# One hybrid diffusion-transformer step: the two softmax maps of a differential head subtracted ahead of the product with the values

## The chip, the cores and the metric

The kernel runs on one core of a Trainium2 chip. The metric is device time in microseconds (us) of one execution. The program of before takes 1923.86 us (median of 3 runs, 1923.54 to 1925.37).

## What is computed

One inference step of a two-layer backbone on 128 context tokens and 512 latent tokens, model width 1024. Layer 0 mixes eight heads of latent attention (MLA) with four heads of differential attention; layer 1 mixes grouped-query and neighbourhood attention. Each layer ends with a gated feed-forward part of width 2816. The change lies in the differential heads. Their reference, cut to what matters (head of two 64-wide query and key halves c, values 128 wide, per-head norm behind):

```python
def diff_attend(q, k, v, lam):
    scale = q.shape[-1] ** -0.5
    def block(qb):
        s = jnp.einsum('bqhcd,bthcd->bhcqt', qb, k).astype(jnp.float32) * scale
        p = jax.nn.softmax(s, axis=-1)
        a = (p[:, :, 0] - lam * p[:, :, 1]).astype(v.dtype)
        return jnp.einsum('bhqt,bthd->bqhd', a, v)
    return map_query_blocks(block, q)
```

The latents (512 queries) read 640 keys, five tiles of 128. The context tokens read only context tokens, in a separate small part that the change leaves as it is.

## The kernel before

Attention of layer 0 is `attention("att0", ...)` over eight jobs, each a pair of maps: D0 to D3 are the four differential heads (a pair is the two maps of a head), M0 to M3 are pairs of MLA heads. Iteration i of its loop works on three pairs side by side: the maxima of pair i+1 (`max_steps`: PE writes a product into PSUM as `pm`, DVE reduces it, L503), the scores of pair i (`score_steps`: PE writes transposed scores `st`, key tile by 512 queries, L546; ACT writes their exponentials into `p`, two key tiles to one 128x1024 tile, or `ps` for the fifth tile, L558; POOL adds the five tiles of a map into `ac`, L562 and L565), and the values of pair i-1 (`value_steps`, PE, L615). The order on each engine follows the order of the calls, with a tile framework's own scheduling on top: each iteration has six stages, and in each come two maxima, a sixth of the scores, one step of the values (the string 'xxsv' of `CFG`), then a step of the list `lag` and a piece of the adaLN products (`ada`, L300 and L307), which are fillers.

For a differential head before, both maps have a value product of their own: `po` of map 0 and of map 1, five products each of a 128x128 by 128x512 tile in f32, each of which the trace shows as two matmul records. `fin` copies both with ACT (L624, and L629 into the tile `dt`). Softmax sums come one or two iterations after the values: `norm_steps`, once for D0 and D1 and once for D2 and D3, makes the sums `su` on PE with the weights `ones` (L643), inverts them on DVE (L650), splits the reciprocals into a high and a low part (ACT L160, DVE L161), spreads them to all partitions with PE (`bcast`, `bc`, L658 and L659, 128x512), multiplies `o` and `dt` by them (L666, L667) and adds minus lambda times the second to the first (L668). The per-head norm of the output (`pr.after`: `sub` with the parts `ps_sub` L248, `pc_sub` L265, `pb_sub` L273 on PE, then L1065 and L1066 on DVE) follows on the same list.

PSUM has two kinds of tiles here: `pmm` (two banks: `pm`, `st`, `qs`) and `psm` (one bank: `po`, `su`, `bc`, `qt`, `qo`, the parts of `sub`, `ada`); all come from one pool of eight banks, given out in the order of the calls. The weight tiles `wt` (`wr`, `wm`, `wh`, `wl`, twelve buffers) hold streamed weights elsewhere in the program and `p` and `ac` in the attention.

```python
            for m, mp in enumerate(pr.maps):
                pj, s, e = mp.p[kt]
                out = pr.po[m] if pr.diff else pr.po[0][64 * m : 64 * m + 64]
                PE.matmul(out[:, s:e], mp.v(kt), pj, start=(i == 0), stop=(i == 4))
```

Of the kernel before, what the change touches and what calls it, by code (L numbers as in the profile page):

```python
# [35 lines left out]
WMB = 4  # L36
# [20 lines left out]
def tile_step(ctx: ExitStack, tc: tile.TileContext, a: dict):  # L57
# [23 lines left out]
    def psm(name, kind="sm"):  # L81
        """One bank of PSUM; kinds may share a ring, each phase of the step in its own way."""
        tag, bufs = banks[kind]
        return pq.tile([128, 512], F32, tag=tag, name=name, bufs=bufs)
# [7 lines left out]
    def place(shape):  # L92
        """A view of the tile that stays."""
# [10 lines left out]
    def ring(tag, cols, bufs, dt=F32):  # L104
        """The next of a ring of views of the tile that stays."""
# [7 lines left out]
    def wt(tag, name, dt=F32):  # L113
        if tag in ("k4", "rope32"):
            return dr(name, dt)[:, 0:1024]
        return rp.tile([128, 1284], dt, tag=tag, name=name, bufs={"wr": 2, "wm": WMB}.get(tag, 3))[:, 0:1024]
# [15 lines left out]
    # ---------------------------------------------------------------- constants  # L132
# [11 lines left out]
    # ---------------------------------------------------------------- projections  # L144
# [24 lines left out]
    def halves(pt, m=128, e=0, cut=HALF):  # L169
        """The two banks of a pair hold the halves so that all 640 columns, and e more before them, are contiguous."""  # L170
        return pt[:m, 512 - cut - e : 512], pt[:m, 512 : 512 + NT - cut]
# [21 lines left out]
    def proj_pair(pts, wss, xs, e, cut):  # L193
        """Two chunks whose first halves come before their second halves."""
# [10 lines left out]
    def chunks(items, u, first_pair):  # L205
        """items: (weights, name, evacuate) per chunk of 128 columns over the model width."""
# [18 lines left out]
    # ---------------------------------------------------------------- norms  # L225
# [3 lines left out]
    class Sums:  # L229
        """Sums of squares over features: chunk i of total accumulates in psum quadrant i % 4."""  # L230
# [48 lines left out]
    # ---------------------------------------------------------------- adaLN  # L279
# [6 lines left out]
    def adaln_steps(l, b, wide=False):  # L286
        """256 columns of w_mod: a fourth of the rows of each half sits in each column tile of the array."""
# [25 lines left out]
    def adaln(l, v):  # L313
        """One of the six vectors: shift, scale, gate of the mixer, then of the ffn."""
# [5 lines left out]
    def mod_scale(l, i, c0=0, c1=8):  # L320
        """A = norm_w * (1 + scale) of sub-layer i (0: attention, 1: ffn)."""
# [3 lines left out]
    def mod_gate(l, i):  # L325
        """G = gate * norm_w of the norm after sub-layer i."""
# [3 lines left out]
    def regions(cut):  # L330
        """Both parts of the tokens, split by kind."""
# [5 lines left out]
    def square_h(h, hf, cut, name):  # L337
        """Sums of squares of a part of the residual stream."""
# [9 lines left out]
    def residual(h, y, ysums, hf, cut):  # L348
        """h += y / rms of a part of the tokens, where y has its gate already; y is lost."""
# [32 lines left out]
    class Raw:  # L382
        """The scaled residual stream before its norm, after the shifts of both kinds of tokens as two
        columns: a product with it times the reciprocal root mean square, plus the product of the
        shift, is the product with the modulated norm."""
# [30 lines left out]
    # ---------------------------------------------------------------- start: residual stream, first adaLN group  # L416
# [35 lines left out]
    # ---------------------------------------------------------------- small vectors  # L452
# [17 lines left out]
    def lam_column():  # L470
        """-lambda = exp(l2 . l3) - exp(l0 . l1) - lambda_init on every partition."""
# [19 lines left out]
    # ---------------------------------------------------------------- attention of a pair of maps  # L491
    def max_steps(pr):
        """Row maxima of the scores of a pair of maps, negated, into their query tiles."""
# [11 lines left out]
        def near(m, qts):  # L505
            """Two query tiles with as many keys: context keys, then those of the neighbourhood with their bias."""
# [1071 lines left out]
def _masks():  # L1578
# [4 lines left out]
    out = []  # L1583
# [125 lines left out]
```

## Time and profile before

| what | value |
|---|---|
| median of 3 runs | 1923.86 us |
| range of the runs | 1923.54 to 1925.37 us |
| span of the profiled execution | 2037.7 us (28995 instructions) |
| PE busy | 1983.5 us, 97% |
| PE weight loads busy | 1666.1 us, 82% |
| DVE busy | 1016.9 us, 50% |
| ACT busy | 799.6 us, 39% |
| POOL busy | 206.1 us, 10% |
| mean granted clock of PE | 0.836 |

The profiled execution has no time of its own beside its span; its span is 1.059 times the median of the runs. A duration of the trace becomes a duration of a run by the inverse of that, 0.944. Busy shares are means over the whole program; attention of layer 0 lies between about 200 and 440 us of the span, its differential heads between about 245 and 355 us, and the rows behind the prediction come mostly from there. In the views, a PE row such as "x4 2.18" groups four matmul records that follow each other and 2.18 us from the first start to the last end; the cost of the group is the distance to the start of the next row. A bracket behind a row gives how long the engine was idle before it and what ended that.

### The profile page before, as it was taken

To read this page: it belongs to the slowest core of one execution; us is meant where nothing else is said; L and a number is where in the kernel's file an instruction comes from. 1 tells how busy PE (TensorE), PEld (TensorE's weight loads), DVE (VectorE), ACT (ScalarE), POOL (GpSimd) and SP (SyncE) were. 2 spreads that over 40 slices of the span, in tenths; PEclk is the share of its full clock that TensorE was granted. 3 is DMA by queue.
4 is the path that set the end of the run, shared out by engine and by line. 5 is a ranking of instruction groups with operands and counts; after the bars stand their busy time and mean duration, and the time that the engine had idled before them with its cause. 6 is when DMAs were issued, how large, how long until landed. Compare 5 with 4: busy or idle time off the path is not lost. (4 is left out here: it accounts for less than half of the span.)

```text
span 2037.7 us, 28995 instructions
## 1 busy us (share of the span) xinstructions
PE 1983.5 (97%) x11715; PEld 1666.1 (82%) x11715; DVE 1016.9 (50%) x1776; ACT 799.6 (39%) x1325; POOL 206.1 (10%) x205
## 2 busy tenths in 40 slices
PE   7999799999999999999999999999999999999997
PEld 4888555568799999999978985456879999999995
DVE  3353554463664563653645543435266456365454
ACT  3432233244543442442465422324364344144243
POOL 0010243330100000000010003630010000000000
PEclk7888788888888888888888887888888888888887
DMA  7445654242212324332323354573322221311221
GB/s 267 160 155 185 169 138 117 63 165 94 83 64 88 112 73 151 109 105 92 110 72 130 112 172 149 151 205 106 116 83 82 75 93 41 105 58 58 80 71 52
DMA packets 84103, 229.89 MB, mean 113 GB/s; under 512 B 12225, under 2 KB 24897, under 8 KB 83969
## 3 DMA queue, kind: packets, MB, share of 16 engines
q1 hardware_dynamic: 74656, 209.73, 32.6%
q10 hardware_dynamic: 6720, 7.82, 1.4%
q0 software_dynamic: 2592, 10.49, 1.3%
q8 instruction: 92, 1.51, 0.3%
q14 instruction: 43, 0.34, 0.1%
HBM read 198.82 MB, written 28.06 MB: 111 GB/s over the span
## 5 line engine op out<-in xcount | busy, mean ns | idle before, releaser
L186 PE MATMUL pu<-uop,wh_u 128*128 128x322 f32 (+1 forms) x2688 | 536.0, 323 | 0.0
L186 PEld LDWEIGHTS pu<-uop,wh_u 128*128 128x128 f32 x2688 | 445.9, 193 | 6.6 <-issue 5.2
L186 PE MATMUL pu<-uop,wl_u 128*128 128x322 f32 x1344 | 322.7, 323 | 0.0
L1333 DVE SCALAR_TENSOR_TENSOR za<-za,cst 128x127 f32<-128x127 f32 (+1 forms) x528 | 193.1, 435 | 96.7 <-ACT za L1325 96.6
L186 PEld LDWEIGHTS pu<-uop,wl_u 128*128 128x128 f32 x1344 | 233.5, 191 | 0.0
L186 PE MATMUL dn<-g,wh_d 128*128 128x320 f32 x1088 | 215.8, 323 | 0.0
L186 PEld LDWEIGHTS dn<-g,wh_d 128*128 128x128 f32 x1088 | 179.8, 192 | 1.0 <-issue 1.0
L269 POOL TENSOR_TENSOR cst<-cst 128x3 f32<-128x3 f32 (+2 forms) x23 | 23.7, 1032 | 1299.2 <-DVE cst L267 1295.9
L414 ACT ACTIVATE za<-za,cst 128x128 f32<-128x128 f32 (+1 forms) x176 | 89.3, 555 | 111.0 <-DVE za L412 102.0
L160 ACT ACTIVATE wh_u<-wr_u 128x1024 fp32r<-128x1024 f32 x88 | 92.1, 1052 | 102.8 <-PE dn L186 55.3
L186 PE MATMUL dn<-g,wl_d 128*128 128x320 f32 x544 | 130.4, 322 | 0.0
L161 DVE TENSOR_TENSOR wl_u<-wr_u,wh_u 128x1024 fp32r<-128x1024 f32 x84 | 102.2, 1217 | 22.7 <-ACT wh_u L160 22.6
L186 PEld LDWEIGHTS dn<-g,wl_d 128*128 128x128 f32 x544 | 94.7, 191 | 0.0
L411 DVE COPY cst<-pu 128x2 f32<-128x2 f32 x88 | 13.9, 158 | 160.2 <-PE pu L186 154.6
L1325 ACT ACTIVATE za<-za,cst 128x640 f32<-128x640 f32 x88 | 81.2, 923 | 2.9
L160 ACT ACTIVATE g<-za 128x640 fp32r<-128x640 f32 x44 | 32.5, 739 | 123.4 <-DVE za L1364 123.4
L1380 DVE TENSOR_TENSOR yf<-yf,dn 128x640 f32<-128x640 f32 x32 | 26.3, 821 | 105.4 <-PE dn L186 105.4
L160 ACT ACTIVATE wh_d<-wr_d 128x768 fp32r<-128x768 f32 (+1 forms) x48 | 38.0, 803 | 90.6 <-PE dn L186 71.7
L412 DVE TENSOR_TENSOR za<-pu,rnuop 128x640 f32<-128x640 f32 x88 | 71.7, 815 | 0.0
L300 PE MATMUL ada<-wm,cst 128*32 128x256 f32 x768 | 68.7, 436 | 2.0 <-ACT psD L558 1.2
L1359 ACT ACTIVATE za<-za 128x640 f32<-128x640 f32 x44 | 32.5, 739 | 94.1 <-DVE za L1333 94.1
L161 DVE TENSOR_TENSOR wl_op<-wr_op,wh_op 128x1024 fp32r<-128x1024 f32 x26 | 31.7, 1223 | 69.1 <-ACT wh_op L160 63.7
(579 smaller groups left out, 3595.4 us busy)
## 6 DMA issues: line engine op xcount, KB each, us to landing
wm<-in_wmod SPq DMA_DIRECT2D x96, 512.0 KB
wr_u<-in_w_up SPq DMA_DIRECT2D x88, 512.0 KB
wr_op<-in_w_o SPq DMA_DIRECT2D x26, 512.0 KB
wr_d<-in_w_dn SPq DMA_DIRECT2D x32, 384.0 KB
wr_dl<-in_w_dn SPq DMA_DIRECT2D x24, 320.0 KB
wr_d<-in_w_dn SPq DMA_DIRECT2D x16, 320.0 KB
h<-in_xT SPq DMA_DIRECT2D x4, 640.0 KB
hb<-in_xT SPq DMA_DIRECT2D x4, 640.0 KB
```

Of the source, the lines that this page charges most:

```text
L160: ACT.activation(hi, src, AF.Copy)
L161: low.tensor_tensor(lo, src, hi, op=ALU.subtract)
L186: PE.matmul(o[hf], w, xhalf(x, hf, e), start=start, stop=stop)
L269: POOL.tensor_tensor(r[:, :nt], ms[:, :nt], mhalf.to_broadcast([128, nt]), op=ALU.pow)
L300: PE.matmul(st["pt"][32 * j : 32 * j + 32, 0:256], silu_c[:, 4 * r + j, :], st[r][:, j * 256 : (j + 1) * 256], start=(r == 0), stop=(r == 1))
L411: DVE.tensor_copy(zb, pt[:, 510 - cut : 512 - cut])
L412: DVE.tensor_tensor(dst, pview(pt, cut=cut), self.r, op=ALU.mult)
L414: ACT.activation(dst[:, s:e], dst[:, s:e], AF.Identity, bias=zb[:, ty : ty + 1])
L1325: ACT.activation(acc, z, AF.Identity, scale=cw[:, 1:2], bias=cw[:, 3:4])
L1333: DVE.scalar_tensor_tensor(acc[:, d0 : d0 + n], z[:, s0 : s0 + n], w, acc[:, d0 : d0 + n], op0=ALU.mult, op1=ALU.add)
L1359: ACT.activation(t[0], t[0], AF.Silu)
L1380: DVE.tensor_tensor(yv, yv, pview(pt), op=ALU.add)
```

## The change

For a differential head the two exponentiated maps are combined before the value product. With E the exponentials of map 0 and F those of map 1, and s and t their sums over keys, the result is (1/s) times V^T (E - lambda (s/t) F). The step `ratio`, ahead of the five value steps, makes the sums of this one pair (eight f32 matmuls of 128 columns into four row quadrants, L654), the reciprocal (L656), minus lambda s/t (L657), the split (L160, L161), spreads the ratio to all partitions (`spread`, eight matmuls of 128x128 columns, L641 and L642) and combines the fifth key tile; `comb(0)` and `comb(1)` combine key tiles 0 and 1, and 2 and 3, ahead of the value steps that read them first. Each `comb` is a product (L665, one operand in PSUM) and a sum of two tiles in SBUF (L666) on DVE. One `po` is left, with five value products (L616), one ACT copy, and a product by the spread 1/s on DVE (L627). `norm_steps` isn't called for differential heads; the per-head norm goes on the list `lag` at the end of the iteration of the values, so it runs in the next iteration, one head in each, where before it ran for two heads together. Tiles `wt` are 1024 columns wide in place of 1284. Comments are taken out too, which shifts line numbers by some 30 behind the attention.

```diff
     def wt(tag, name, dt=F32):
...
-        return rp.tile([128, 1284], dt, tag=tag, name=name, bufs={"wr": 2, "wm": WMB}.get(tag, 3))[:, 0:1024]
+        return rp.tile([128, 1024], dt, tag=tag, name=name, bufs={"wr": 2, "wm": WMB}.get(tag, 3))
...
-                pr.po = [psm(f"po{pr.name}{m}", "po") for m in range(2 if pr.diff else 1)]
+                pr.po = [psm(f"po{pr.name}", "po")]
...
-            for m, mp in enumerate(pr.maps):
+            for m, mp in enumerate(pr.maps[:1] if pr.diff else pr.maps):
                 pj, s, e = mp.p[kt]
-                out = pr.po[m] if pr.diff else pr.po[0][64 * m : 64 * m + 64]
+                out = pr.po[0] if pr.diff else pr.po[0][64 * m : 64 * m + 64]
...
         def fin():
             ACT.activation(pr.of[:, 128:640], pr.po[0], AF.Copy)
             if pr.diff:
-                if pr.idx % 2 == 0:
-                    group["tmp"] = dr(f"dt{pr.name}")
-                pr.tmp = group["tmp"][:, 512 * (pr.idx % 2) : 512 * (pr.idx % 2) + 512]
-                ACT.activation(pr.tmp, pr.po[1], AF.Copy)
-
-        return [lambda i=i: one(i) for i in range(5)], fin
+                DVE.tensor_tensor(pr.of[:, 128:640], pr.of[:, 128:640], spread(pr, 0), op=ALU.mult)
+
+        steps = [lambda i=i: one(i) for i in range(5)]
+        if pr.diff:
+            cs = comb_steps(pr)
+            steps = [cs[0]] + [lambda i=i: (cs[i + 1](), one(i)) if i < 2 else one(i) for i in range(5)]
+        return steps, fin
+
+    def spread(pr, half):
+        pb = psm(f"bc{pr.name}{half}")
+        for q in range(4):
+            o, c = pb[:, 128 * q : 128 * q + 128], slice(128 * half, 128 * half + 128)
+            sl = sel2[:, 256 + q : 257 + q].to_broadcast([128, 128])
+            PE.matmul(o, sl, pr.att.rh[:, c], start=True, stop=False)
+            PE.matmul(o, sl, pr.att.rl[:, c], start=False, stop=True)
+        return pb
+
+    def comb_steps(pr):
+        st = {}
+        def ratio():
+            ps = psm(f"su{pr.name}")
+            for m, mp in enumerate(pr.maps):
+                for q in range(4):
+                    PE.matmul(ps[32 * q : 32 * q + 32, 128 * m : 128 * m + 128], ones, mp.acc[:, 128 * q : 128 * q + 128], start=True, stop=True)
+            rc = pr.att.rc[:, 0:256]
+            DVE.reciprocal(rc, ps[:, 0:256])
+            DVE.scalar_tensor_tensor(rc[:, 128:256], ps[:, 0:128], nlam, rc[:, 128:256], op0=ALU.mult, op1=ALU.mult)
+            split(rc, pr.att.rh[:, 0:256], pr.att.rl[:, 0:256])
+            st["r"] = spread(pr, 1)
+            comb(2)
+        def comb(g):
+            x, y = (mp.pd[g] for mp in pr.maps)
+            n = x.shape[1]
+            DVE.tensor_tensor(y, y, st["r"].unsqueeze(1).to_broadcast([128, n, 512]), op=ALU.mult)
+            DVE.tensor_tensor(x, x, y, op=ALU.add)
+        return [ratio, lambda: comb(0), lambda: comb(1)]
...
         def scale(g):
...
-            if pr.diff:
-                DVE.tensor_tensor(x, x, bcast(2 + 2 * g, f"{pr.name}a"), op=ALU.mult)
-                DVE.tensor_tensor(pr.tmp, pr.tmp, bcast(3 + 2 * g, f"{pr.name}b"), op=ALU.mult)
-                DVE.scalar_tensor_tensor(x, pr.tmp, nlam, x, op0=ALU.mult, op1=ALU.add)
-            else:
-                DVE.tensor_tensor(x, x, bcast(g, pr.name), op=ALU.mult)
+            DVE.tensor_tensor(x, x, bcast(g, pr.name), op=ALU.mult)
...
-        for pr in prs:
-            if pr.after:
-                out += pr.after
         return out
...
-            if i >= 3 and i % 2 == 1:
+            if i >= 3 and i % 2 == 1 and not prs[i - 3].diff:
                 lag += norm_steps([prs[i - 3], prs[i - 2]])
...
                         if s == 5 and vfin:
                             vfin()
+                            if prs[i - 1].diff:
+                                lag += prs[i - 1].after
```

How this moves the work is seen best in iteration 2, where the scores are those of D2, the values those of D1 and the maxima those of D3. On PE, before, from the first maximum of D3 (`poD10` and `poD11` are the products of the two maps of D1):

```order
L502 MATMUL pmD300_1984<-q010_1462 128x320 x2
L307 MATMUL ada011_1927<-cst_69 128x2 x2
L502 MATMUL pmD301_1988<-q010_1462 128x320 x2
L615 MATMUL poD10_2002<-psD1_1831,vd2_1304 128x512
L546 MATMUL stD200_1994<-q014_1660 128x512
L615 MATMUL poD11_2003<-psD1_1831,vd2_1304 128x512
L502 MATMUL pmD302_2010<-q010_1462 128x320 x2
L615 MATMUL poD10_2002<-pD100_1838,vd0_1302 128x512
```

On PE, after, the same stretch of the program, first its beginning and then, behind the left-out rows, its first value products (`bcD11` is the spread ratio of D1):

```order
L654 MATMUL suD1_2036<-acD1_1832,cst_69 32x128 x8
L248 MATMUL ps_sub0_1998<-cst_69 32x320 x2
L502 MATMUL pmD300_2018<-q010_1462 128x320 x2
L265 MATMUL pc_sub0_2061<-cst_69 128x1 x5
L502 MATMUL pmD301_2022<-q010_1462 128x320 x2
L641 MATMUL bcD11_2049<-att1_1460,sel2_491 128x128
L546 MATMUL stD200_2028<-q014_1660 128x512
...
L273 MATMUL pb_sub0_2069<-cst_69 128x128 x5
L642 MATMUL bcD11_2049<-att1_1460,sel2_491 128x128
...
L502 MATMUL pmD302_2081<-q010_1462 128x320 x2
L502 MATMUL pmD303_2085<-q010_1462 128x320 x2
...
L616 MATMUL poD1_2100<-psD1_1831,vd2_1304 128x512
```

The first value product stands behind the sums, the norm of D0 (`sub0`), the spread, four score products to each of two tiles (the left-out `st` rows) and four maxima, where before it stood behind two maxima.

On DVE, after, in the same iteration:

```order
L656 RECIPROCAL att0_1459<-suD1_2036 128x256
L657 SCALAR_TENSOR_TENSOR att0_1459<-suD1_2036,cst_69,att0_1459 128x128
L503 TENSOR_REDUCE cst_69<-pmD300_2018 128x1
L267 TENSOR_SCALAR cst_69<-pc_sub0_2061 128x5
L503 TENSOR_REDUCE cst_69<-pmD301_2022 128x1
L161 TENSOR_TENSOR att1_1460<-att0_1459,att1_1460 128x256
L1096 TENSOR_TENSOR o0_2_1461<-o0_2_1461,pb_sub0_2069 128x640
L1097 TENSOR_SCALAR o0_2_1461<-o0_2_1461,cst_69 128x640
L665 TENSOR_TENSOR psD1_1831<-psD1_1831,bcD11_2049 128x512
L503 TENSOR_REDUCE cst_69<-pmD302_2081 128x1
L666 TENSOR_TENSOR psD1_1831<-psD1_1831 128x512
```

The two operations of the norm of D0 (L1096, L1097), which wait for `pb_sub0`, stand ahead of the first product of the combination (L665). Before, this stretch of DVE held only the four maxima, and three small operations of the adaLN part.

## Rows read from the trace of the kernel before

**Rows 1.** windows, attention of layer 0: us, each engine busy (records), PEclk, DMA, GB/s
```profile
250.00:442.00 192.00, 190.75 (x859) 102.19 (x858) 98.62 (x153) 66.88 (x113) 78.64 (x60) 0.84 0.39 112
```

**Rows 2.** timeline of PE: start us, us; two value products
```profile
261.64 2.18 PE L615 MATMUL poD<-pD,vd 128*128 128x512 f32 x4
263.75 0.70 PE L300 MATMUL ada<-wm,cst 128*32 128x256 f32 x8
```

**Rows 3.** timeline of PE, 307 to 341 us: scores, spreads, the norm of D0
```profile
307.36 3.15 PE L546 MATMUL stD<-q 128*128 128x512 f32 x10
311.70 0.67 PE L300 MATMUL ada<-wm,cst 128*32 128x256 f32 x8 [1.19 <-ACT psD L558]
...
312.70 0.43 PE L659 MATMUL bcD0a<-att,sel 128*128 128x512 f32 x1
312.94 0.43 PE L658 MATMUL bcD0b<-att,sel 128*128 128x512 f32 x1
...
317.08 1.42 PE L248 MATMUL ps_sub<-cst 128*32 128x320 f32 x4
318.43 0.56 PE L502 MATMUL pmM<-q 96*128 96x320 f32 x2
...
320.51 1.39 PE L265 MATMUL pc_sub<-cst 32*128 32x1 f32 x10
...
340.12 1.42 PE L273 MATMUL pb_sub<-cst 128*128 128x128 f32 x10
```

**Rows 4.** timeline of PE: the softmax sums of the differential heads
```profile
295.10 1.19 PE L643 MATMUL suD<-acD,cst 128*32 128x512 f32 x8
...
357.63 1.14 PE L643 MATMUL suD<-acD,cst 128*32 128x512 f32 x2
...
360.38 1.15 PE L643 MATMUL suD<-acD,cst 128*32 128x512 f32 x6
```

**Rows 5.** timeline of PE: short matmuls of adaLN
```profile
382.33 1.19 PE L300 MATMUL ada<-wm,cst 128*32 128x256 f32 x16
```

**Rows 6.** timeline of PE: first and last of nine 128x128 matmuls
```profile
142.14 0.22 PE L166 MATMUL pkc<-ckvl,uqk 128*128 128x128 f32 x1
...
143.06 0.30 PE L167 MATMUL pkc<-ckvh,uqk 128*128 128x128 f32 x1
```

**Rows 7.** lines of DVE, 240 to 442 us: busy us, mean ns, idle before
```profile
L503 DVE TENSOR_REDUCE cst<-pmD 128x1 f32<-128x640 f32 x16 | 13.0, 821 | 10.3 <-PE pmD L502 10.2
...
L650 DVE RECIPROCAL att<-suD 128x256 f32<-128x256 f32 x4 | 7.0, 1755 | 6.0 <-PE suD L643 6.0
...
L700 DVE TENSOR_TENSOR att<-att,cst 128x256 f32<-128x256 f32 x7 | 4.6, 652 | 0.1
...
L1065 DVE TENSOR_TENSOR o<-o,pb_sub 128x640 f32<-128x640 f32 x4 | 3.3, 821 | 8.4 <-PE pb_sub L273 8.4
...
L161 DVE TENSOR_TENSOR wl_op<-wr_op,wh_op 128x1024 fp32r<-128x1024 f32 x2 | 2.4, 1222 | 2.4 <-PE poM L615 2.4
L1066 DVE TENSOR_SCALAR o<-o,cst 128x640 f32<-128x640 f32 x4 | 2.2, 547 | 0.1
```

**Rows 8.** timeline of DVE, the end of the differential heads before
```profile
313.77 0.68 DVE L667 TENSOR_TENSOR dtD<-dtD,bcD0b 128x512 f32<-128x512 f32 x1
314.48 1.62 DVE L668 SCALAR_TENSOR_TENSOR o<-dtD,cst,o 128x512 f32<-128x512 f32 x1
...
317.40 0.75 DVE L668 SCALAR_TENSOR_TENSOR o<-dtD,cst,o 128x512 f32<-128x512 f32 x1
```

**Rows 9.** timeline of POOL: the last addition of the exponentials of D3
```profile
314.28 1.28 POOL L565 TENSOR_TENSOR acD<-acD,psD 128x512 f32<-128x512 f32 x1
```

**Rows 10.** windows around a fall of PEclk, and around 311 us
```profile
94.00:95.00 1.00, 0.58 (x3) 0.29 (x3) 0.12 (x1) 0.00 (x0) 0.80 (x1) 0.85 0.81 283
95.00:102.00 7.00, 6.86 (x27) 6.40 (x28) 2.95 (x7) 1.36 (x2) 0.91 (x2) 0.51 0.38 93
...
310.00:312.00 2.00, 0.81 (x11) 0.21 (x9) 0.59 (x1) 1.64 (x3) 1.71 (x2) 0.85 0.00 0
```

More of the change, by code (lines that the diff above doesn't have):

```diff
@@ L539, in setup @@
             for m, mp in enumerate(pr.maps):
-                mp.p = {}
+                mp.p, mp.pd = {}, []
                 mp.acc = None if pr.na else accs[:, 512 * m : 512 * m + 512]
@@ L558, in dense @@
             ACT.activation(pd, pt[:, 0 : nk * 512], AF.Exp, scale=pr.scale)
+            mp.pd.append(pd.rearrange("p (a b) -> p a b", a=nk))
             for kk in range(nk):
@@ L656, in bcast @@
             pb = psm(f"bc{name}")
-            sl = sel2[:, blk * 128 : (blk + 1) * 128] if blk < 2 else sel2[:, 254 + blk : 255 + blk].to_broadcast([128, 128])
+            sl = sel2[:, blk * 128 : (blk + 1) * 128]
             PE.matmul(pb, sl, rh, start=True, stop=False)
```

## The prediction, made before the changed kernel was run

> **What bounds the kernel now.** I read the page first: PE is busy 97% of the span, so time moves only if PE's work or PE's waits move. Then the windows, to see whether that holds where the change is: in attention of layer 0 PE is busy 190.75 of 192.00 us, DVE 98.62, POOL 78.64 [rows 1]. The stretch is PE's, and waits make up 1.25 us of it, nearly all one wait of 1.19 for ACT's last exponential of D3 [rows 3]. DVE is half idle, but it reduces the maxima in order and waits for PE before many of them (10.3 us in 16 maxima of the differential heads, [rows 7]): its slack is spread in small pieces. Then PE's timeline for the price of each product, DVE's lines for its operations, and POOL's timeline for when a map's sum is complete.
>
> A result within 0.2% (3.9 us) of 1923.86 counts as no change; a measurement of this kernel can't tell less. The sum below is in us of the profiled execution, span 2037.7; the median of the runs is 0.944 of it, and I scale at the end.
>
> **PE's work taken away.** Two value products take 2.11 from start to the next row [rows 2], so 1.055 each. Four heads lose five each: 20 x 1.055 = 21.1. The spreads of before are 16 matmuls (four to a head) at 0.24, the step between two of them [rows 3]: 3.9. The sums of before take 1.19, 1.14 and 1.15 in three pieces [rows 4], less the few hundredths that each runs into the next: 3.3. Together 28.3.
>
> **PE's work added.** Per head eight sum matmuls of 128 columns. Before, one quadrant had 512 columns in 1.1 us; now it has 256, so by columns 0.55. By instructions, they are 16 records, and 16 short records of adaLN take 1.19, with the next row some 0.07 ahead of that end [rows 5]: 1.1. I take 1.1, since that row shows what many short records take; 0.55 stays as the other end. Four heads: 4.4. The spreads are 64 matmuls of 128 columns; nine such stand 0.115 apart [rows 6], so 7.4. Net of PE's work: 28.3 - 11.8 = **-16.5**.
>
> **ACT.** Four copies go. Nothing waited for them at length; they are hidden under PE, and the cover stays. Counted 0.
>
> **DVE's work.** Per head it gains a product and a sum of 512 columns (0.68 and 0.75, [rows 8]), two products and two sums of 1024 columns (no row with one operand in PSUM at that size; the sum of two SBUF tiles takes 1.22 [rows 7], twice 0.68 would be 1.36; I take 1.22), the product in `fin` (0.68) and the small ratio (under 0.65, the row of 256 columns; I take 0.4). That is 7.4, less 0.68 + 0.68 + 0.75 that go: +5.3 per head, 21 in all. DVE goes from 99 to some 120 of 192: no bound by its share. What counts is where it stands: the value products, which waited for ACT alone, now wait for DVE.
>
> **The new waits.** I walked iteration 2 through the two orders, t = 0 at the end of D1's sums. DVE: reciprocal 1.75 [rows 7], ratio 0.4. PE meanwhile: `ps_sub0` 1.35, a maximum about 0.5, then `pc_sub0`, which needs a bank that the sums still hold for DVE and ACT: a wait of about 0.4. Then `pc_sub0` 1.3, a maximum, a first spread, four scores at 0.315 and `pb_sub0` 1.3 [rows 3]: PE is at 6.7. DVE's order now puts the two operations of the norm (0.82 and 0.55, [rows 7]), which wait for `pb_sub0`, ahead of the first product of the combination. So DVE ends product, a maximum (0.82) and sum at 6.7 + 1.37 + 0.68 + 0.82 + 0.75 = 10.3, and PE, with the other spreads, two maxima and four scores, is at the first value product at 9.8: it waits 0.5. Onward in the same way, with a maximum and 1.22 + 1.22 and a small context operation on DVE against a product, short adaLN matmuls and a maximum on PE: 0.6 at key tile 0. For key tiles 2 and 3 DVE has two maxima, 2 x 1.22 and some 1.4 of context operations (5.5), PE two products, a maximum, scores and two more maxima (4.2): 1.3. Sum 2.8.
>
> Ahead of that stands the wait of the sums for POOL. The last score of D3 ended at 310.51 [rows 3] and its last addition at 315.56 [rows 9]: 5.05. Before, the sums came far later; now PE has only a value product (1.05), the spread of the pair before (0.9), a context product (0.3) and the half of the sums that reads the other map (0.55) to cover it, and the adaLN matmuls between the scores, some 0.9, that let POOL catch up. 5.05 - 3.7 = 1.3. Iteration 2 so costs 4.1. Iterations 1 and 3 look alike; in iteration 4 the scores are those of M0, in three passes for two, and cover more: 2.4 (estimate, the half of the DVE part gone). Sum 3 x 4.1 + 2.4 = **+14.7**. Bounds: no wait at all, 0, if the orders on the chip drift in DVE's favour, to 20 if each POOL wait is the full 5.05 less the value product and the spread, 3.
>
> **The lock between DVE and POOL.** The combination's sum reads two SBUF tiles. At 314.48 such an operation began 0.20 into a POOL addition (314.28 to 315.56), and took 1.62 in place of 0.75 [rows 8, 9]: it ended 0.54 after POOL's end. Twelve new sums meet POOL, which is busy 78.64 of 192 (41%), and lose half an addition when they do: 12 x 0.41 x 0.64 = **+3.1**; between 0 and 12 x 1.28 = 15.4.
>
> **A wait that goes.** The 1.19 at 311.70 [rows 3] was PE at a short adaLN matmul behind the scores of D3; that place now has the spread of D2 ahead of it: **-1.2**. If it stays, the sum is 1.2 higher.
>
> **The granted clock.** At 94 us PE was busy 0.58 of 1 us, among short matmuls, and over the next 7 us the granted clock was 0.51 (the lower level, 1.2 GHz) where it had been 0.85 (the upper, 2.4 GHz); at 310 to 312 PE was busy 0.81 of 2 and the clock stayed at 0.85 [rows 10]. A fall costs 7 x (1 - 0.51/0.85) = 2.8. Each of the four stretches from the sums to the first product now has short matmuls (sums, spreads) among waits of 0.4 to 1.3. One such row fell and one did not, so I take two falls of four: **+5.6**; bounds 0 and 11.2.
>
> The Trainium skill (TensorE: Matmul & The Clock Gate, section "A second HAM failure mode: psum-queue depth-cycling") tells of a kernel whose PE idled briefly between groups of matmuls so often that its clock went back and forth; by it all four would fall, which is the case "clock" below. The row at 310 speaks against it, the row at 94 for it.
>
> **Trimmed buffers.** `wt` gives back 1040 bytes of each of twelve buffers in a partition. No row shows PE waiting for such a buffer, and the orders outside attention stay nearly as they were: 0. Some loads on SP's queue and one spill on POOL's move by a few places; PE waits for none of them in the rows: 0.
>
> **Sum.** -16.5 + 14.7 + 3.1 - 1.2 + 5.6 = +5.7 of the profile, x 0.944 = +5.4: 1929 us.
>
> **Rivals.**
> *Covered* (faster): DVE stays ahead of PE, because its idle pieces lie where the combination stands. It decides at the first value product: if DVE's L666 ends before PE's last score of that stage, only the POOL waits, 4 x 1.3, remain, with no falls of the clock: -16.5 - 1.2 + 5.2 = -12.5, so 1912; without those too, 1907. For it: DVE at 62%, and PE almost without waits before. Against: the operations of the norm that now stand ahead of the first product. Chance 0.24.
> *Even*: waits as walked, but the clock stays up, as at 310: 5.7 - 5.6, 1924. Chance 0.22.
> *Clock* (slower): all four stretches fall: 5.7 + 5.6 = 11.3, 1934.5. Chance 0.10.
> *Lock* (slower): DVE's sums and POOL's additions run in step, since both follow the scores, and each of the twelve waits a whole addition: 5.7 + 15.4 - 3.1 = 18.0, so 1941. It decides where the three sums of a head stand beside POOL's five additions to a map. For it: the row at 314.48; against: POOL is free 59% of the time. Chance 0.07. The Trainium skill (SBUF — State Buffer, "Summary: rules for kernel authors") says that a VectorE operation with two SBUF inputs and a GpSimd operation that reads SBUF exclude each other, the second waiting until the first ends; the row of 1.62 agrees.
>
> **Numbers.** The forecast, 1924 to 1934 around 1929, has the rest, 0.37. Below 1920.0 lies *covered* with a little of *even* and of the forecast: 0.31. Between 1920.0 and 1927.7 most of *even* and some of the forecast: 0.24. Above: 0.45. For 8 in 10 the range runs from inside *covered* to the edge of *lock*: 1910 to 1940.
>
> **What would show it.** In the profile after: five L616 products per head at 1.055; PE idle before L616 released by DVE L666, 0.5 to 1.3 at a time; idle at the sums L654 released by POOL L565, about 1.3; PEclk at 0.5 in two of the stretches from L654 to the first L616; DVE's L666 with a maximum near twice its median. I am wrong if PE is still busy over 99% there (*covered*), if the waits sit at the maxima's banks in place of the products, or if the time changed outside attention of layer 0.

## The result, and the profile after

The changed kernel takes 1948.24 us (median of 4 runs, 1947.19 to 1950.77) against 1924.61 for the kernel before: 1.0121 times as long, interval 1.0103 to 1.0140, so 23.6 us **slower**. The forecast had the sign, and put it at 1929 with a range that ended at 1940: the time lies outside.

The page of the changed kernel, first the span, then busy time by engine, then the granted clock in 40 slices:

```profile
span 1947.3 us, 29086 instructions
...
PE 1870.2 (96%) x11771; PEld 1591.2 (82%) x11771; DVE 1040.4 (53%) x1796; ACT 804.8 (41%) x1321; POOL 207.2 (11%) x205
...
PEclk8999788999999999999999998999999999999999
```

Span and granted clock show a trap at once. This profile ran at a mean clock of 0.972; that of before, on which the prediction rests, at 0.836, and its span of 2037.7 lay 6% over its runs. The two spans can't be compared. So the kernel before was profiled once more, as the first run below (clock 0.981, span 1922.5), and from here on "before" is that profile. Its windows, ahead of the differential heads' value products, around them and behind them (columns as in [rows 1]):

```profile
200.00:252.00 52.00, 40.19 (x199) 25.48 (x198) 28.73 (x46) 16.70 (x29) 21.35 (x19) 0.80 0.66 178
252.00:352.00 100.00, 98.47 (x477) 53.80 (x479) 52.94 (x87) 32.09 (x55) 38.73 (x31) 1.00 0.51 147
352.00:440.00 88.00, 86.75 (x466) 56.79 (x466) 46.71 (x59) 37.81 (x61) 30.66 (x22) 1.00 0.35 130
```

The same windows of the changed kernel:

```profile
200.00:252.00 52.00, 38.49 (x177) 25.08 (x175) 30.73 (x45) 12.30 (x20) 15.56 (x14) 0.67 0.61 169
252.00:352.00 100.00, 84.78 (x459) 54.72 (x458) 64.33 (x93) 28.26 (x48) 35.31 (x27) 0.86 0.43 121
352.00:440.00 88.00, 86.87 (x431) 49.26 (x431) 48.82 (x68) 36.73 (x60) 40.03 (x30) 1.00 0.29 95
```

Between 252 and 352 us PE idles 15.2 us in place of 1.5, and its granted clock is 0.86 in place of 1.00. A mean of 0.86 is a mix of two levels, 1.00 (2.4 GHz) and 0.50 (1.2 GHz): (1 - 0.86)/0.5 of the stretch, some 28 us, went by at the lower one. Ahead of 252 us it is 34 us in place of 21. Behind 352 the two are alike.

Where attention ends is told by the first product with the output weights, start of the first and of the last at the end of the row, before and then after:

```profile
L186 PE MATMUL op<-oh,wh_op x96: 302/308/416, 411.3 to 436.0; 128*128 128x320 f32 x96
```

```profile
L186 PE MATMUL op<-oh,wh_op x96: 303/309/421, 435.0 to 459.8; 128*128 128x320 f32 x96
```

That start moves by 23.7 us, and what follows it is 1511.2 us before and 1512.3 after. The loss lies ahead of that product, nearly all of it in attention of layer 0.

**A balance.** What PE does in a time at the lower clock takes twice as long (a value product of the changed kernel took 1.87 us from 285.37 to the next row at the lower clock; before, two took 1.81 at the upper). So the end of attention should be PE's work (all else up to that point) plus idle plus half of the time at the lower clock. The rows behind this, two value products of the kernel before and then one of the changed kernel, each with the row behind it:

```profile
246.38 1.88 PE L615 MATMUL poD<-pD,vd 128*128 128x512 f32 x4
248.19 0.64 PE L300 MATMUL ada<-wm,cst 128*32 128x256 f32 x8
...
285.37 2.08 PE L616 MATMUL poD<-pD,vd 128*128 128x512 f32 x2 [2.02 <-DVE pD L666]
287.24 0.42 PE L739 MATMUL qtD<-cst,att 128*128 128x128 f32 x1
```

Idle and clock are summed over windows of 4 us from 200 to 440 us, for every kernel profiled; "end" is the start of that first product with the output weights, and all but the run time is in us of the profile:

| kernel | end | idle | lower clock | work = end - idle - half of lower | run time |
|---|---|---|---|---|---|
| before | 411.3 | 14.6 | 20.5 | 386.4 | 1924.3 |
| changed | 435.0 | 29.9 | 61.5 | 374.4 | 1948.2 |
| no combination | 415.9 | 21.7 | 41.0 | 373.7 | 1931.1 |
| late norms | 425.3 | 24.8 | 61.5 | 369.8 | 1936.2 |
| wide tiles | 432.0 | 32.8 | 47.8 | 375.3 | 1947.0 |
| fill | 436.9 | 29.0 | 27.4 | 394.2 | 1953.2 |
| shift | 418.8 | 23.5 | 47.8 | 371.4 | 1936.2 |
| sums on PE | 427.3 | 22.7 | 64.9 | 372.2 | 1944.2 |
| work given back | 446.1 | 27.5 | 58.2 | 389.5 | 1964.1 |
| no wait for POOL | 419.2 | 27.0 | 30.6 | 376.9 | 1933.7 |
| neither | 403.7 | 16.7 | 23.9 | 375.1 | 1918.9 |
| shift by two | 432.3 | 27.8 | 51.2 | 378.9 | 1943.4 |
| probe | 418.6 | 14.4 | 20.5 | 394.0 | 1929.8 |

For the change: work -12.0, idle +15.3, half of the lower clock +20.5, together the 23.7 seen. That they close proves nothing, because the work column is what is left over. What can be tested is whether it behaves like PE's work: it holds within some 5 us of its mean, 374, for the eight kernels that do the same on PE, 20 value products given back (18 us by their rows) show as 15, and the sums of the probe (3 us) as 8. So each split is good to about 5 us. Idle inside a stretch at the lower clock is counted in both columns; that is 9 to 12 us in every kernel, and shifts a comparison by less than 2. The balance rests on one profile each, and the run times of the variants spread over 2 to 12 us.

Who PE waited for, 252 to 352 us of the changed kernel, the five longest (us in total, times, longest):

```profile
PE suD L654 <- POOL acD L566: 5.3, 3, 2.0
PE poD L616 <- DVE pD L666: 5.1, 4, 2.1
PE poD L616 <- DVE psD L666: 1.8, 2, 1.1
PE pmD L502 <- ACT psD L558: 1.1, 2, 0.7
PE pc_sub L265 <- DVE att L657: 0.8, 1, 0.8
```

And iteration 2, the one that the prediction walked, on PE:

```profile
264.89 0.43 PE L654 MATMUL suD<-acD,cst 128*32 128x128 f32 x8 [1.60 <-POOL acD L566]
265.13 1.24 PE L248 MATMUL ps_sub<-cst 128*32 128x320 f32 x4
...
267.68 1.24 PE L265 MATMUL pc_sub<-cst 32*128 32x1 f32 x10 [0.81 <-DVE att L657]
...
270.45 1.38 PE L273 MATMUL pb_sub<-cst 128*128 128x128 f32 x10
...
275.26 1.12 PE L616 MATMUL poD<-psD,vd 128*128 128x512 f32 x2 [1.14 <-DVE psD L666]
```

with DVE in the same stretch:

```profile
265.38 1.76 DVE L656 RECIPROCAL att<-suD 128x256 f32<-128x256 f32 x1 [1.94 <-PE suD L654]
...
271.87 0.82 DVE L1096 TENSOR_TENSOR o<-o,pb_sub 128x640 f32<-128x640 f32 x1 [1.27 <-PE pb_sub L273]
272.73 0.56 DVE L1097 TENSOR_SCALAR o<-o,cst 128x640 f32<-128x640 f32 x1
273.20 0.68 DVE L665 TENSOR_TENSOR psD<-psD,bcD 128x512 f32<-128x512 f32 x1
...
283.02 2.29 DVE L666 TENSOR_TENSOR pD<-pD,pD 128x1024 f32<-128x1024 f32 x1
```

The chain is there as walked: `pb_sub` on PE, then the norm of the head before on DVE, then the first product of the combination, then PE's value product. PE's next wait, 2.02 us for the last row, is the start of a fall of the clock: the windows from 284 to 296 and 296 to 312 us have a granted clock of 0.72 and 0.68.

```profile
284.00:296.00 12.00, 10.55 (x55) 6.58 (x55) 5.07 (x9) 4.55 (x9) 3.86 (x4) 0.72 0.22 53
296.00:312.00 16.00, 13.74 (x58) 10.48 (x58) 8.50 (x13) 3.56 (x5) 4.24 (x5) 0.68 0.49 154
312.00:320.00 8.00, 6.35 (x39) 3.56 (x38) 7.88 (x11) 1.40 (x3) 3.27 (x3) 1.00 0.47 155
```

### The profile page after: what moved, and what is told of

Same layout as the page of the kernel before. It is cut to its first block, busy times and chain, and to the rows that moved or that the text cites. A ratio compares the mean times of both kernels' runs of the same rounds, so it can differ in the third digit from the quotient of the medians.

```text
span 1947.3 us, 29086 instructions
## 1 busy us (share of the span) xinstructions
PE 1870.2 (96%) x11771; PEld 1591.2 (82%) x11771; DVE 1040.4 (53%) x1796; ACT 804.8 (41%) x1321; POOL 207.2 (11%) x205
## 4 chain that ended last, share of the span: by engine, by line
PE 79%; issue 7%; DVE 4%; POOL 2%; ACT 1%; DMA 1%; ACTq 1%; SPq 0%; DVEq 0%; POOLq 0%
PE pu L186 31%; PE dn L186 12%; PE ada L300 2%; PE poG L616 1%; PE pnq L186 1%; PE stM L546 1%; PE op L186 1%; PE stG L546 1%; PE pqc L186 1%; PE pnk L186 1%; PE poM L616 1%; PE poD L616 1%; PE op L166 1%; PE op L165 1%; PE op L167 1%
## 5 line engine op out<-in xcount | busy, mean ns | idle before, releaser
L186 PE MATMUL pu<-uop,wh_u 128*128 128x322 f32 (+1 forms) x2688 | 512.7, 312 | 0.0
L186 PEld LDWEIGHTS pu<-uop,wh_u 128*128 128x128 f32 x2688 | 428.7, 190 | 5.8 <-ACT wh_u L160 4.1
L186 PE MATMUL pu<-uop,wl_u 128*128 128x322 f32 x1344 | 308.5, 311 | 0.0
L186 PEld LDWEIGHTS pu<-uop,wl_u 128*128 128x128 f32 x1344 | 224.9, 188 | 0.0
L186 PE MATMUL dn<-g,wh_d 128*128 128x320 f32 x1088 | 204.2, 309 | 0.0
L186 PEld LDWEIGHTS dn<-g,wh_d 128*128 128x128 f32 x1088 | 170.9, 188 | 0.8 <-ACT wh_d L160 0.8
L269 POOL TENSOR_TENSOR cst<-cst 128x3 f32<-128x3 f32 (+2 forms) x23 | 23.7, 1032 | 1226.6 <-DVE cst L267 1221.0
L160 ACT ACTIVATE wh_u<-wr_u 128x1024 fp32r<-128x1024 f32 x88 | 93.0, 1059 | 135.0 <-PE dn L186 68.9
L186 PE MATMUL dn<-g,wl_d 128*128 128x320 f32 x544 | 124.3, 309 | 0.0
L161 DVE TENSOR_TENSOR wl_u<-wr_u,wh_u 128x1024 fp32r<-128x1024 f32 x84 | 102.4, 1218 | 20.6 <-ACT wh_u L160 20.5
L160 ACT ACTIVATE wh_d<-wr_d 128x768 fp32r<-128x768 f32 (+1 forms) x48 | 38.5, 808 | 109.1 <-PE dn L186 98.6
L160 ACT ACTIVATE g<-za 128x640 fp32r<-128x640 f32 x44 | 32.5, 739 | 115.4 <-DVE za L1395 115.4
L161 DVE TENSOR_TENSOR wl_op<-wr_op,wh_op 128x1024 fp32r<-128x1024 f32 x26 | 31.7, 1223 | 64.5 <-ACT wh_op L160 64.4
L300 PE MATMUL ada<-wm,cst 128*32 128x256 f32 x768 | 63.5, 408 | 2.4 <-DMA wm<-in_wmod 1.7
```

Of the source, the lines that this page charges most:

```text
L160: ACT.activation(hi, src, AF.Copy)
L161: low.tensor_tensor(lo, src, hi, op=ALU.subtract)
L186: PE.matmul(o[hf], w, xhalf(x, hf, e), start=start, stop=stop)
L300: PE.matmul(st["pt"][32 * j : 32 * j + 32, 0:256], silu_c[:, 4 * r + j, :], st[r][:, j * 256 : (j + 1) * 256], start=(r == 0), stop=(r == 1))
```

## The experiments

Theory 1: the loss is PE's new waits, for POOL's last addition and for DVE's combination, and the falls of the granted clock that come with them. Theory 2: it lies outside (trimmed buffers, moved loads). Rival 3: the clock falls because there are many short matmuls, whatever the waits. Rival 4: the lock between DVE and POOL (a sum that begins inside an addition ends only behind it) carries it. A ratio below is against the kernel before timed beside the variant.

**Before, profiled again** (no edit).

> The kernel before, once more, for a profile at the higher granted clock (the profile shown of it ran at 0.836, that of the changed kernel at 0.972). Theory 1 (the changed kernel loses in attention of layer 0, to waits of PE and to falls of the granted clock that follow them): about 1924 us; between 250 and 350 us PE idles under 3 us and the granted clock stays at its upper level, against 15.2 us of idle and some 27 us at the lower level in the changed kernel. Theory 2 (the loss lies elsewhere: the trimmed buffers, the order of loads): the two profiles are alike up to the end of attention of layer 0, and differ behind it.

1924.3 us, one run. The windows above: 1.5 us of idle between 252 and 352, clock 1.00. Theory 2 falls already here, since the profiles part inside attention and run alike behind it.

**No combination.** The value products read the first map's exponentials, so the output lacks the second map.

```diff
             st["r"] = spread(pr, 1)
-            comb(2)
...
-        return [ratio, lambda: comb(0), lambda: comb(1)]
+        return [ratio, lambda: None, lambda: None]
```

> The changed kernel without the combination itself: the products and sums L665 and L666 of the three groups of key tiles are left out, the value products read the exponentials of the first map alone. Sums, ratio, spreads and the order of the rest stay. Theory 1 with DVE as its main cause: PE's waits for L666 (6.9 us) and the falls of the clock behind them go, while the waits for POOL (6.6 us) stay: about 1930 us (1924 to 1935). Theory 1 with POOL as its main cause: over 1940 us. Theory 2: 1945 us or more.

1931.05 us, 1.0028 times before (1.0015 to 1.0042). The waits for L666 are gone, those for POOL stay (252 to 352 us):

```profile
PE suD L654 <- POOL acD L566: 4.5, 3, 1.7
PE pc_sub L265 <- DVE att L657: 1.6, 2, 0.8
```

The combination carries 17 us of the loss: its waits, its meetings with POOL and the falls of the clock behind them, which this run does not separate. With it gone, and some 12 us less of PE's work, the kernel is still not faster than before.

**Late norms.** The norm of two heads together in every second iteration, as before.

```diff
-            if i >= 3 and i % 2 == 1 and not prs[i - 3].diff:
-                lag += norm_steps([prs[i - 3], prs[i - 2]])
+            if i >= 3 and i % 2 == 1:
+                if prs[i - 3].diff:
+                    lag += [lambda: None] * 5 + prs[i - 3].after + prs[i - 2].after
+                else:
+                    lag += norm_steps([prs[i - 3], prs[i - 2]])
...
-                            if prs[i - 1].diff:
-                                lag += prs[i - 1].after
```

> The changed kernel with the per-head norms at their old place, two heads together in every second iteration. Theory 1: pb_sub no longer stands ahead of the first combination, one wait of about 1 us in three iterations goes, and perhaps a fall of the clock: 1940 to 1946 us. If the early norms were the main cause: under 1932 us. Theory 2: no change, 1948 us.

1936.16 us, 1.0054 (1.0035 to 1.0073): 12 us better than the changed kernel, more than expected for theory 1, though not the main cause. The place of the norms is half of the loss, by itself a detail of a list. The balance gives 5 us of it to idle and 5 to a lower work column, which is no more than the balance's error, and none to the clock; so where the 12 us come from is settled only in part.

**Wide tiles.** `wt` at 1284 columns again.

```diff
-        return rp.tile([128, 1024], dt, tag=tag, name=name, bufs={"wr": 2, "wm": WMB}.get(tag, 3))
+        return rp.tile([128, 1284], dt, tag=tag, name=name, bufs={"wr": 2, "wm": WMB}.get(tag, 3))[:, 0:1024]
```

> The changed kernel with the weight tiles 1284 columns wide again. Theory 1: 1948 us, within 3. Theory 2 (the trim costs): 1930 us or less.

1946.97 us, the changed kernel's time: the trim costs nothing.

**Fill.** 64 idle matmuls: ten a head between the sums of its two maps, six ahead of its first value product.

```diff
+                for _ in range(6 if pr.diff else 0):
+                    PE.matmul(pr.po[0][:, 0:128], ident, ident, start=True, stop=True)
...
             for m, mp in enumerate(pr.maps):
+                for _ in range(10 * m):
+                    PE.matmul(ps[:, 384:512], ident, ident, start=True, stop=True)
                 for q in range(4):
```

> The changed kernel with 64 idle matmuls added in the stretches where PE waits: ten products of 128x128 in f32 between the sums of the two maps of a head and six ahead of its first value product, about 15 us of PE work in all, whose results are written over. Theory 1 (PE's waits make the granted clock fall, and the lower clock costs more than the waits): the fill takes the place of most of the 15 us of waits, the clock stays up, about 1930 us. Rival 3 (the clock falls because of the many short matmuls, whatever the waits): more short matmuls, no gain, 1948 to 1963 us.

1953.2 us, a miss by 23 us. The clock stayed up, as theory 1 had it (27.4 us at the lower level, from 61.5), and more short matmuls did not lower it, against rival 3. But idle stayed at 29 us: the scheduler spread the fill over the iteration, the second map's sums came later, and PE then waited for the split of the ratio. By the balance 20 us of work were paid in full, and the clock gave 17 back. As a test of the waits it is inconclusive.

**Shift.** Late norms (that edit is not shown again), the ratio a stage later, the value products two stages behind it, sums into the second map's tile.

```diff
-            DVE.tensor_tensor(x, x, y, op=ALU.add)
+            DVE.tensor_tensor(y, x, y, op=ALU.add)
...
-            for m, mp in enumerate(pr.maps[:1] if pr.diff else pr.maps):
+            for m, mp in enumerate(pr.maps[1:] if pr.diff else pr.maps):
...
-            steps = [cs[0]] + [lambda i=i: (cs[i + 1](), one(i)) if i < 2 else one(i) for i in range(5)]
+            steps = [lambda: None, cs[0], cs[1], lambda: (cs[2](), one(0)), lambda: (one(1), one(2)), lambda: (one(3), one(4))]
```

> The kernel with late norms (1936 us), with the ratio one stage later and the value products two stages behind it, so that POOL's additions and DVE's combinations have a stage of cover each (the last four products share two stages); the sums go into the tile of the second map, so that the first map's buffers come free early. Work on every engine is the same. Theory 1: PE's 8.4 us of idle between 252 and 352 us shrink to under 4, the 31 us at the lower clock there to under 10: 1915 to 1925 us. Rival 3: the clock falls all the same, 1930 us or more.

1936.2 us, no better than late norms: a miss. Idle between 252 and 352 stayed at 8.2 us (8.4 with late norms alone), spread over more causes. The two longest of 252 to 352 us:

```profile
PE suD L654 <- POOL acD L566: 2.5, 2, 1.9
PE pmM L502 <- ACT pD L558: 1.5, 2, 0.8
```

**Sums on PE.** Late norms (not shown again), and the fifth key tile added by PE in the sums in place of POOL.

```diff
-                    PE.matmul(ps[32 * q : 32 * q + 32, 128 * m : 128 * m + 128], ones, mp.acc[:, 128 * q : 128 * q + 128], start=True, stop=True)
+                    o = ps[32 * q : 32 * q + 32, 128 * m : 128 * m + 128]
+                    PE.matmul(o, ones, mp.acc[:, 128 * q : 128 * q + 128], start=True, stop=False)
+                    PE.matmul(o, ones, mp.p[4][0][:, 128 * q : 128 * q + 128], start=False, stop=True)
...
-            else:
+            elif g == 1 or not pr.diff:
```

> The kernel with late norms, with the fifth key tile of a differential head left out of POOL's additions and added by PE in the sums (eight more f32 matmuls of 128 columns per head, about 0.5 us; POOL does one addition of 1.27 us less per map). Theory 1: the 2.4 us of waits for POOL go, and perhaps one fall of the clock: 1928 to 1934 us. Rival 4 (the lock between DVE and POOL carries the loss): 8 fewer additions to meet, each up to 1.27: 1926 us or less.

1944.2 us, slower than late norms by 8: a miss. No wait for POOL is left in its list of waits, but the time at the lower clock was the longest of all (64.9 us): waits for DVE's maxima, the ratio's split and the combination remained. And no sum of the combination met an addition any more (the eight large ones took 1204 to 1220 ns, their least): without the lock the kernel is no faster, so rival 4 falls as the carrier of the loss.

**The work given back.** The changed kernel with the second map's value products, into a bank nobody reads.

```diff
+                if pr.diff:
+                    pr.px = psm(f"px{pr.name}", "po")
...
+            if pr.diff:
+                PE.matmul(pr.px, mp.v(kt), pr.maps[1].p[kt][0], start=(i == 0), stop=(i == 4))
```

> The changed kernel with the removed work given back: five value products of the second map per head into a bank that nobody reads, about 20 us of PE work. Theory 1: the products fill PE's waits and keep the clock up, so that the time grows by far less than 20 us, or falls: 1935 to 1952 us. Rival 3, and any theory in which PE's work counts in full: 1962 to 1970 us.

1964.05 us: 16 us more than the changed kernel, the expectation of the rivals. The products did cover the combination on DVE (no wait of PE for its sums is left), but not POOL, for which PE waited longer (252 to 352 us):

```profile
PE suD L658 <- POOL acD L566: 7.9, 3, 2.9
```

So it was wrong that any work of PE's would serve as cover: the work stood behind the sums, and the wait is ahead of them.

**No wait for POOL.** Both sums from the first map's additions; the ratio is then that of one map with itself.

```diff
-                    PE.matmul(ps[32 * q : 32 * q + 32, 128 * m : 128 * m + 128], ones, mp.acc[:, 128 * q : 128 * q + 128], start=True, stop=True)
+                    PE.matmul(ps[32 * q : 32 * q + 32, 128 * m : 128 * m + 128], ones, pr.maps[0].acc[:, 128 * q : 128 * q + 128], start=True, stop=True)
```

> The changed kernel with the sums of both maps of a differential head taken from the first map's additions (the second map's additions are still made, but nobody waits for them). PE's 6.6 us of waits for POOL go, the waits for DVE stay. By the balance of the runs so far (end of attention = PE's work + idle + half of the time at the lower clock; the changed kernel 374 + 30 + 31, the kernel before 386 + 15 + 10): if the falls of the clock start at the sums, 6.6 us of idle and some 25 us at the lower clock go: 1928 us (1924 to 1934). If they follow the waits for DVE alone: 1940 us or more.

1933.71 us, 1.0049 (1.0029 to 1.0068): 14.5 us of the loss go with 6.6 us of waits. Only 3 us of them show up as less idle (waits for the combination grew by 1.4, and other waits came); the time at the lower clock fell from 61.5 to 30.6.

**Neither.** This edit and that of no combination together; both parts of the computation are left out.

> Both taken away: no combination on DVE and both sums from the first map's additions. By the same balance idle and lower clock come near those of the kernel before (15 and 20 us), and PE's work is 12 us less: 1912 us (1908 to 1918), faster than before. If short matmuls alone make the clock fall (rival 3): 1925 us or more.

1918.88 us, just above the range, and 0.9970 (0.9952 to 0.9988) of before: faster by 6 us. The short matmuls, the spreads and the early norms are all in it, so rival 3 falls as a cause by itself. Idle and lower clock are back at 16.7 and 23.9 us. Its windows:

```profile
252.00:352.00 100.00, 97.14 (x589) 61.80 (x590) 55.61 (x96) 34.58 (x59) 43.70 (x35) 0.98 0.53 151
```

The four kernels make a square: 1948 with both waits, 1931 without DVE's, 1934 without POOL's, 1919 without either. 17.2 and 14.5 add up to 31.7, and 29.4 is measured: the two add, nearly.

**Shift by two.** Shift, with the ratio one stage later still (two behind its place in the changed kernel) and a fourth `wh` buffer (that line is not shown).

```diff
-            steps = [lambda: None, cs[0], cs[1], lambda: (cs[2](), one(0)), lambda: (one(1), one(2)), lambda: (one(3), one(4))]
+            steps = [lambda: None, lambda: None, cs[0], cs[1], lambda: (cs[2](), one(0), one(1)), lambda: (one(2), one(3), one(4))]
```

> A try at a kernel that computes all and beats both: late norms, the ratio two stages later, the value products two stages behind it, the sums in the second map's tile, and a fourth wh buffer from the room that the trim gave. The scores of the pair then run ahead of the sums, POOL's additions are over when they come. If the waits go: PE's work 372 + idle 18 + half of 25: 1915 us (1910 to 1924). If the value products at the end of the iteration now wait for DVE or for ACT's buffers instead: 1930 us or more.

1943.44 us. The waits for POOL are gone. In their place PE's spreads wait for the ratio's split (5.5 us), and its value products and scores still wait for DVE (2.1 and 2.4).

**Probe.** The kernel before, with the sums made also at the changed kernel's place.

```diff
+                if pr.diff:
+                    ps = psm(f"sx{pr.name}")
+                    for m, mp in enumerate(pr.maps):
+                        for q in range(4):
+                            PE.matmul(ps[32 * q : 32 * q + 32, 128 * m : 128 * m + 128], ones, mp.acc[:, 128 * q : 128 * q + 128], start=True, stop=True)
```

> The kernel before with one thing added: the sums of each differential head are also made at the changed kernel's place, ahead of the first value product, into a bank that nobody reads. So PE meets the wait for POOL's last addition, and nothing of the combination. PE's work grows by some 3 us. If a wait of about 2 us per head among short matmuls costs just itself: 1924 + 3 + up to 7 = 1934 us at most, with the time at the lower clock as before (20 us). If the clock falls behind it (what the balance says): 10 to 25 us more at the lower clock, half of it lost: 1936 to 1946 us. If the second value products, which do not depend on the sums but stand behind them in PE's order, keep PE's waits short: under 1930 us.

1929.83 us, 1.0020 (1.0006 to 1.0034). The probe did not meet what it was to measure: PE waited for POOL once, 0.8 us, because value products, maxima and scores stood between the sums of the two maps. The clock was as before (20.5 us at the lower level). It shows that the short sums by themselves cost about 4 us and lower no clock; what a wait for POOL costs alone it leaves open.

No variant that computes all came below the kernel before.

## Why the prediction was wrong

**PE's work, -16.5.** The balance gives -12.0. The durations were taken from a profile at a granted clock of 0.85; at 1.00 two value products take 1.81 from start to next row in place of 2.11 [rows 2]. 0.85 x 16.5 = 14.0, which is inside the balance's error. The common factor 0.944 was wrong in kind: PE's value products scale with its clock, DVE's and POOL's operations don't (a maximum takes 816 and 817 ns in the two profiles of before, an addition 1272 and 1275). The sums were mis-sized too: the two halves of a head take some 0.43 and 0.24, so 0.7 and not 1.1, nearer the count by columns than that by instructions.

**The waits, +14.7 and +3.1, less 1.2.** 16.6 in the sum, 15.3 more idle measured, but that these agree is partly luck. The waits for POOL came out larger: 1.3 walked per head, measured 1.31, 1.60, 1.67 and 1.99. Those for DVE came out smaller, 7.7 in place of some 9.5 and the 3.1 of the lock. Iterations 2 and 3 had about what was walked (2.8): in iteration 2, 0.81 at `pc_sub` (0.4 walked), 1.14 at the first product (0.5), none at key tile 0 (0.6) and 2.02 at key tiles 2 and 3 (1.3), of which 1.08 is the lock. Iterations 1 and 4 had nearly none, 0.39 together; in iteration 1 PE ran at the lower clock from 237 to 250 us while DVE combined. And the wait for ACT's last exponential did not go: it moved from an adaLN matmul (1.2) to the maxima (1.1 and 0.4).

**The lock, +3.1.** The eight large sums L666 take 1208 ns at the least and 1766 in the mean, 4.5 us more in all:

```profile
L666 DVE TENSOR_TENSOR pD<-pD,pD x8: 1208/1852/2289, 244.5 to 351.7; 128x1024 f32<-128x1024 f32 x8
```

Five of the eight began inside a POOL addition, and these are the five long ones. Each ended 1.07 or 1.08 us behind the end of that addition. The two worst take 2.29, at 283.02 and 319.15, and PE's two longest waits for DVE, 2.02 and 2.08, are behind them. The first of the two additions, from 282.88 to 284.23, beside the sum at 283.02 shown above:

```profile
282.88 1.35 POOL L566 TENSOR_TENSOR acD<-acD,psD 128x512 f32<-128x512 f32 x1 [4.93 <-ACT psD L558]
```

The small sums (681 to 686 ns) met nothing. The mechanism and its size were right; in step all the way, as *lock* had it, the two never ran. The Trainium skill (SBUF — State Buffer, "Summary: rules for kernel authors") says that the second of the two waits until the first ends. These rows agree: behind the addition's end a sum still took 1.08 of the 1.21 that it takes alone.

**The clock, +5.6.** This is the step that failed: "One such row fell and one did not, so I take two falls of four", at 2.8 each, with a bound of 11.2. Measured: 41 us more at the lower clock, 20.5 us lost. The fall ahead of the value products, which both kernels have, was over by 228 us in both. Behind it the changed kernel's clock fell six times: at 237, 285, 298, 322, 332 and 339 us. Three of the four stretches from the sums to the first product had a fall, the last of them two; in iteration 2 the clock stayed up there, across waits of 1.60 and 0.81. Two falls lay where the prediction had put none, at the waits for key tiles 2 and 3. Five of the six began during a wait of PE of 1.3 to 2.1 us or within 2 us behind it; the sixth, at 339, began while PE was busy with the norm and the scores.

The price of one fall was less wrong. The six lasted 6.8 us in the mean, near the 7 of [rows 10]; each cost half of its length, since the upper level was 1.00, where the forecast reckoned 0.4 from 0.85. They were uneven, from some 3 to nearly 14 us, and the two longest were not drawn out by new waits, since PE was busy without a break from 238 and from 299 us on:

```profile
240.00:244.00 4.00, 4.00 (x23) 2.28 (x22) 1.80 (x3) 0.00 (x0) 0.00 (x0) 0.50 0.00 0
...
300.00:304.00 4.00, 3.99 (x16) 3.55 (x16) 1.55 (x4) 0.76 (x2) 0.92 (x1) 0.50 0.94 307
```

Much of what PE did in these two were the short matmuls of the spreads, adaLN and the norm, so rival 3 may have a part in how long a fall lasts; no run separates that. The rival *clock* had the mechanism, but its four falls, 11.2, are still half of what was lost. The page named there (the Trainium skill, TensorE: Matmul & The Clock Gate, "A second HAM failure mode: psum-queue depth-cycling") tells of a clock that goes back and forth when PE often idles briefly. The trace agrees for five of the six falls.

**Trimmed buffers, ACT, the rest of the program: 0.** Right: wide tiles give the same time, and what follows attention differs by 1 us.

The forecast's own rows gave -14 + 16.6, some 3 us slower than before. So without the clock they say no change, and the sign rested on the term that was sized worst. What separates them from the 23.6 measured is the clock, 20.5 by the balance.

## What to carry to other kernels

Taking work off the bounding engine pays only if its order has something ready to put in the gaps; here 12 us of products were traded for sums, a ratio and a combination that stand in one chain over POOL, PE and DVE, inside a stage whose pieces were full. Price each new wait of PE twice, once for itself and once for the clock behind it: in this kernel 15 us more of idle came with another 20 lost to the clock. And before durations are taken from a profile, hold its granted clock and span against the runs: here PE's value products scaled with the clock, the operations of DVE and POOL didn't.

## What was not expected of the hardware

Two profiles of the kernel before ran at upper levels of 0.85 and 1.00, with spans of 2037.7 and 1922.5 us; the runs, at 1924, go with the second. And the waits' cost was nearly additive (17.2 and 14.5, together 29.4), though by the balance the falls of the clock carry more than half of it and are neither regular nor equally long.
